# Shifting the start addresses of TensorE's operands in the feed-forward layers, by 64 bytes from set to set and 32 bytes from pair to pair

## The chip, the cores and the metric

The kernel runs on one core of a Trainium2 chip. The metric is the device time of one execution in microseconds (us). Before the change it is 2165.8 us, the median of two runs (2165.64 and 2165.96).

## What is computed

A trunk of two decoder layers over 256 tokens of width 2048, in float32. Cut to what matters here:

```python
for layer in range(2):
    hn = rms_norm(h, norm_mix[layer])
    h = h + (mlstm_mixer(hn, ...) if layer == 0 else rglru_mixer(hn, ...))
    hn = rms_norm(h, norm_ffn[layer])
    g, u = split(hn @ ffn_w_in[layer])          # 2048 x 11264
    h = h + (silu(g) * u) @ ffn_w_out[layer]    # 5632 x 2048
return rms_norm(h, norm_final)
```

Every product is a matrix of 256 tokens times a weight matrix that is read from HBM once.

## The kernel before

**Two halves of each operand.** TensorE multiplies in the type fp32r, which keeps fewer bits than float32. So each operand is split into a rounded part and a rest: ScalarE casts the raw value into the high half, VectorE subtracts that from the raw value and writes the low half (`split`, L205 to L207). A product is then three matmuls into the same PSUM bank: high by high, high by low, low by high (`block`, L258 to L260; `product`, L687 to L689; `mm_feat`, L275 to L277). The operand that lies still in the array while the other streams through it (the stationary one) is loaded by an LDWEIGHTS instruction ahead of each matmul.

**The feed-forward layer** (`ffn`, L671) runs over four chunks of hidden columns, of 3, 3, 3 and 2 blocks of 512. For each block, `hidden(j)` (L691) streams 8 weight tiles, called pairs p = 0 to 7 (`pairs`, L227). Five of them are plain: 24 matmuls of 512 columns each. Three (p = 1, 3, 5, `SEVENS`) use a scheme with seven products instead of eight, after sums of weights and of operands: 21 matmuls each. Behind each chunk `project_out` (L422) multiplies the block of hidden values with the second weight matrix, in four quarters q of 512 columns, through `linear_tok` (L250) and `stream4` (L215). In both, the weights are the moving operand (512 columns, 2048 bytes in each partition), and the tokens the stationary one (128 columns, 512 bytes).

**Where the operands lie.** `four` (L202) takes each of these weight tiles from a pool: 4 raw buffers, and 3 buffers each for the high halves (`whi`, and `whix` and `whit` for the seven products) and the low halves (`wlo`, `wlox`, `wlot`). All are 4 x 512 elements of 4 bytes, 8192 bytes in each partition, and follow one another. The stationary operands of `hidden` are written by `NormPairs.pair` (L374) into tiles `p0` to `p7` of 6144 or 7168 bytes (`p_f` in the profile). Those of `project_out` are `hh` and `hl`, written by `turn_v` (L732). The mixers have their own weight buffers, from the pool's tags in `stream` (L180), and their own stationary operands (`x_m`, `yh`, `yl`, `zh`, `zl`).

**What orders the work.** The program text gives the order on each engine; casts and subtractions of the weights are put ahead by a priority (`AHEAD`). Buffers in a pool rotate, and a writer waits until the last reader of the buffer is done. Work for the next stage (transposes, statistics) is kept in the list `pending` and taken out one at a time between weight tiles (`run_pending`, L175).

Of the kernel before, what the change touches and what calls it, by code (L numbers as in the profile page):

```python
# [8 lines left out]
F32 = mybir.dt.float32  # L9
F32R = mybir.dt.float32r  # L10
# [4 lines left out]
P = 128  # L15
T = 256
# [8 lines left out]
NB = 512  # L25
EPS = 1e-6
BIG = 1e30
AHEAD = 1000

SEVENS = (1, 3, 5)  # L30
PRODUCTS = (
# [7 lines left out]
def kernel(  # L39
# [23 lines left out]
    small = ctx.enter_context(tc.tile_pool(name="small", bufs=2))  # L63
# [14 lines left out]
    def pool_of(key):  # L78
        return pools[key][0]

    def acc(name):
        return pool_of("acc").tile([P, NB], F32, tag="bank", name=name)
# [67 lines left out]
    part, at, used = 0, 0, [0, 0, 0]  # L150
    for name, src, n in par_src:
        if part == 0 and at or at + n > P:
            part, at = part + 1, 0
# [26 lines left out]
    def stream(w, c0, nk, ncols=NB):  # L180
# [5 lines left out]
        for kg in range(0, nk, 2):  # L186
# [12 lines left out]
            for i in range(2):  # L199
                yield kg + i, hi[:, i, 0:ncols], lo[:, i, 0:ncols]  # L200

    def four(what, name, dtype, bufs):  # L202
        return pool_of("w").tile([P, 4, NB], dtype, tag=what, name=f"{what}{name}", bufs=bufs)

    def split(hi, lo, src):  # L205
        nc.scalar.copy(hi, src)  # L206
# [43 lines left out]
    def linear_tok(w, c0, nk, act, name, ncols=NB, lag=0):  # L250

        ps = [acc(f"{name}_{b}") for b in range(NT)]

        def block(b, k, hi, lo):
            ah, al = act(k)
            bs = slice(b * P, (b + 1) * P)
            o = ps[b][:, 0:ncols]
            nc.tensor.matmul(o, lhsT=ah[:, bs], rhs=hi, start=(k == 0), stop=False)  # L258
            nc.tensor.matmul(o, lhsT=ah[:, bs], rhs=lo, start=False, stop=False)  # L259
            nc.tensor.matmul(o, lhsT=al[:, bs], rhs=hi, start=False, stop=(k == nk - 1))  # L260

        late = []
        for k, hi, lo in stream(w, c0, nk, ncols):
            block(0, k, hi, lo)
            late.append((k, hi, lo))
            if len(late) > lag:
                block(1, *late.pop(0))
            if k > 1:
                run_pending()
        for kt in late:  # L270
            block(1, *kt)
        return ps
# [20 lines left out]
    class Norm:  # L293
# [62 lines left out]
        def finish(self):  # L356
            v = small.tile([P, NT], F32, tag="ms", name=f"ms_{self.name}")
            nc.vector.tensor_reduce(out=v, in_=self.ss, axis=mybir.AxisListType.X, op=ALU.add)
            nc.vector.tensor_scalar(out=v, in0=v, scalar1=1.0 / D, scalar2=EPS, op0=ALU.mult, op1=ALU.add)
            self.rstd = small.tile([P, NT], F32, tag="rstd", name=f"rstd_{self.name}")  # L360
            nc.gpsimd.tensor_tensor(self.rstd, v, mhalf[:, 0:NT], op=ALU.pow)
            if self.bcast:
                dg = small.tile([P, NT, P], F32, tag="dg", name=f"dg_{self.name}", bufs=1)
                for b in range(NT):
                    nc.vector.tensor_scalar_mul(dg[:, b, :], ident, self.rstd[:, b:b + 1])
                pb = misc(f"bc_{self.name}")
                nc.tensor.matmul(pb[:, 0:T], lhsT=ones, rhs=dg.rearrange("p b t -> p (b t)"), start=True, stop=True)
                self.bc = small.tile([P, T], F32, tag="rbc", name=f"rbc_{self.name}")
                nc.scalar.copy(self.bc, pb[:, 0:T])

    class NormPairs(Norm):


        def pair(self, p):  # L374
            plain = p not in SEVENS
            k0, k1 = 2 * p, 2 * p + 1
            order = ((k0, 0), (k0, 1), (k1, 0), (k1, 1)) if plain else ((k1, 1), (k0, 0), (k0, 1), (k1, 0))
            n = 6 if plain else 7
            pt = misc(f"tr_{self.name}{p}").rearrange("p (s t) -> p s t", t=P)
            for i, (k, b) in enumerate(order):  # L380
                nc.tensor.transpose(pt[:, i, :], h[:, b, k * P:(k + 1) * P], ident)
            c = pool_of("x").tile([P, 8, P], F32, tag="c", name=f"c_{self.name}{p}")
            for k, sl in ((k0, slice(0, 2)), (k1, slice(2, 4))) if plain else ((k0, slice(1, 3)), (k1, slice(0, 4, 3))):
                nc.scalar.activation(c[:, sl, :], pt[:, sl, :], AF.Copy, scale=self.gain[:, k:k + 1])
            if plain:
                nc.vector.tensor_tensor(c[:, 4:6, :], c[:, 0:4:2, :], c[:, 1:4:2, :], op=ALU.subtract)
                src = c[:, 0:6, :]
            else:

                nc.vector.tensor_tensor(  # L390
                    c[:, 4:6, :], c[:, 0:1, :].broadcast_to([P, 2, P]), c[:, 2:4, :], op=ALU.subtract
                )
                nc.vector.tensor_tensor(c[:, 6, :], c[:, 3, :], c[:, 4, :], op=ALU.subtract)
                nc.vector.tensor_tensor(c[:, 7, :], c[:, 1, :], c[:, 6, :], op=ALU.subtract)
                src = c[:, 1:8, :]
            xt = pool_of("x").tile([P, 2, n, P], F32R, tag=f"p{p}", name=f"p{p}_{self.name}")
            split(xt[:, 0], xt[:, 1], src)
            self.x.append(xt)

# [22 lines left out]
    def project_out(w, nk, act, nxt, last=True):  # L422

        for q in range(4):
            held = last and q == 3 and nxt.lag
            ps = linear_tok(w, q * NB, nk, act, f"po{q}", lag=nxt.lag if held else 0)
            for b in range(NT):
                hs = h[:, b, q * NB:(q + 1) * NB]
                nc.vector.tensor_tensor(hs, ps[b], hs, op=ALU.add)
                if held:  # L430
                    nxt.store(b)
            if last and q == 0:
                nxt.open()
            if last and not held:
                pending.extend(nxt.parts(q))
# [235 lines left out]
    def ffn(layer, n, nxt):  # L671

        w = ffn_w_in[layer]
# [10 lines left out]
        if True:  # L684
# [5 lines left out]

            def hidden(j):  # L691

                ps = {c: acc(f"{c}_{j}") for c, _, _ in PRODUCTS}
                started = set()
                dif = fp.tile([P, 2, NB], F32, tag="dif", name=f"dif{j}")
                sg = fp.tile([P, NT, NB], F32, tag="sg", name=f"sg{j}")
                for p, ops in pairs(w, j):
                    if p not in SEVENS:

                        for c, side, a in (("Q5", 1, 1), ("P2", 0, 0), ("Q3", 1, 2), ("P4", 0, 1)):  # L700
                            for f in range(2):
                                product(ps[c], n.plain(p, f)[a], ops[2 * side + f], c not in started,
                                        p == NK // 2 - 1 and f == 1)
                                started.add(c)
                    else:
                        seven = n.seven(p)
                        for c, a, b in PRODUCTS:
                            product(ps[c], seven[a], ops[b], c not in started,
                                    p == SEVENS[-1] and c in ("P7", "P1", "Q6"))
                            started.add(c)  # L710
                    if p == SEVENS[-1]:
                        nc.scalar.copy(sg[:, 0, :], ps["P1"])
                        nc.vector.tensor_tensor(dif[:, 0, :], ps["Q6"], sg[:, 0, :], op=ALU.subtract)
                        nc.vector.tensor_tensor(dif[:, 1, :], ps["P7"], dif[:, 0, :], op=ALU.add)
                    if p > 0:
                        run_pending()
                v = fp.tile([P, NT, NB], F32, tag="v", name=f"v{j}")
                for b in range(NT):
                    nc.vector.tensor_tensor(v[:, b, :], ps["Q5"], dif[:, b, :], op=ALU.add)
                nc.vector.tensor_tensor(sg[:, 0, :], ps["P2"], sg[:, 0, :], op=ALU.add)  # L720
                nc.scalar.activation(sg[:, 0, :], sg[:, 0, :], AF.Silu, scale=n.rstd[:, 0:1])
                nc.vector.tensor_tensor(v[:, 0, :], ps["Q3"], v[:, 0, :], op=ALU.add)
                nc.vector.tensor_tensor(sg[:, 1, :], ps["P4"], dif[:, 1, :], op=ALU.subtract)
                nc.scalar.activation(sg[:, 1, :], sg[:, 1, :], AF.Silu, scale=n.rstd[:, 1:2])
                for b in range(NT):
                    nc.vector.scalar_tensor_tensor(
                        out=v[:, b, :], in0=v[:, b, :], scalar=n.rstd[:, b:b + 1], in1=sg[:, b, :],
                        op0=ALU.mult, op1=ALU.mult,
                    )
                return v  # L730
# [38 lines left out]
    nc.vector.tensor_scalar_mul(nsp8, sp8, -1.0)  # L769

    n3 = NormPairs("f1", par["g_ffn"][:, 16:32])

    def rglru_mixer():
        rg = open_pool("rg", "rg")
# [187 lines left out]
```

## Time and profile before

| | |
|---|---|
| time of the profiled execution | 2165.18 us |
| its span, first to last instruction | 2163.4 us |
| median of the runs shown | 2165.8 us |
| TensorE (PE) busy | 2126.7 us, 98% of the span, 10658 matmuls |
| VectorE (DVE) busy | 1524.6 us, 70% |
| ScalarE (ACT) busy | 1071.0 us, 50% |
| DMA | 405.70 MB, mean 188 GB/s |

The span of the profiled execution is the time between its first and last instruction; 1.8 us of its time lie around it. Matmuls are pipelined: one starts while the one before still drains, so the durations of the rows (some 390 ns for 512 columns) overlap, and what a matmul costs is the distance from its start to the next one's start. That distance is read from the timeline, which gives each instruction's start.

### The profile page before, as it was taken

The numbers are of one execution on the slowest core, as the hardware profiler recorded it, in microseconds if no ns is written. First come the engines' busy times: TensorE is split into PE (matmuls) and PEld (weight loads), VectorE is DVE, ScalarE is ACT, GpSimd is POOL, SyncE is SP. The second block draws the span as 40 slices with busy tenths as digits, with TensorE's granted clock in tenths as the row PEclk, the third lists the DMA queues.
The fourth block names the chain that finished last, engine by engine and source line by source line (L and its number), as shares of the span: only waits on it lengthen the run. The fifth ranks groups of instructions, "written<-read, shape, count | busy, mean of one in ns | idle before, by whom it ended". The sixth has DMA issues, their size and how long they took to land.

```text
span 2163.4 us, 26826 instructions
## 1 busy us (share of the span) xinstructions
PE 2126.7 (98%) x10658; PEld 1788.9 (83%) x10658; DVE 1524.6 (70%) x1486; ACT 1071.0 (50%) x1040; POOL 43.4 (2%) x62
## 2 busy tenths in 40 slices
PE   8999999899999999999999999989999999999998
PEld 7988888788888888888879999778888888888886
DVE  5655555688578758866856786768857875886685
ACT  5444445555345435544544758555434543553444
POOL 0011110000000000000000000000000000000002
PEclk9999999999999999999999999999999999999999
DMA  6556655556555655565636665555665565556563
GB/s 209 166 163 178 180 180 185 178 202 209 189 193 188 203 186 195 195 201 188 206 106 195 194 188 188 190 176 195 214 195 194 175 214 175 194 195 213 176 214 117
DMA packets 211078, 405.70 MB, mean 188 GB/s; under 512 B 14520, under 2 KB 14728, under 8 KB 210824
## 3 DMA queue, kind: packets, MB, share of 16 engines
q1 hardware_dynamic: 210808, 402.94, 57.2%
q8 instruction: 83, 1.36, 0.3%
q10 hardware_dynamic: 144, 1.05, 0.1%
q14 instruction: 43, 0.35, 0.0%
HBM read 401.84 MB, written 2.10 MB: 187 GB/s over the span
## 4 chain that ended last, share of the span: by engine, by line
PE 91%; DVE 3%; ACT 2%; DMA 2%; issue 1%; SPq 0%; POOL 0%; ACTq 0%; DVEq 0%; POOLq 0%
PE po L259 10%; PE po L258 10%; PE po L260 10%; PE P L688 7%; PE P L689 7%; PE P L687 7%; PE Q L688 6%; PE Q L689 6%; PE Q L687 6%; DMA raw<-in_ffn_w_in_dram 2%; PE rec L277 1%; PE qk L275 1%; DVE wlo L207 1%; PE qk L276 1%; PE rec L276 1%; PE o L260 1%
## 5 line engine op out<-in xcount | busy, mean ns | idle before, releaser
L206 ACT CAST whi<-raw 128x2048 fp32r<-128x2048 f32 x198 | 378.3, 1912 | 465.8 <-PE P L689 204.4
L207 DVE TENSOR_TENSOR wlo<-raw,whi 128x2048 fp32r<-128x2048 f32 x198 | 451.8, 2295 | 204.8 <-ACT whi L206 204.6
L196 DVE TENSOR_TENSOR wlo<-raw,whi 128x1024 fp32r<-128x1024 f32 (+1 forms) x225 | 273.3, 1219 | 194.0 <-ACT whi L195 193.7
L195 ACT CAST whi<-raw 128x1024 fp32r<-128x1024 f32 (+1 forms) x225 | 234.3, 1047 | 215.8 <-PE po L260 53.2
L259 PE MATMUL po<-wlo,hh 128*128 128x512 f32 x704 | 275.2, 391 | 0.0
L258 PE MATMUL po<-whi,hh 128*128 128x512 f32 x704 | 275.0, 391 | 0.0
L260 PE MATMUL po<-whi,hl 128*128 128x512 f32 x704 | 273.6, 390 | 0.0
L206 ACT CAST whit<-sum 128x2048 fp32r<-128x2048 f32 x66 | 126.2, 1913 | 161.5 <-PE P L689 94.5
L207 DVE TENSOR_TENSOR wlot<-sum,whit 128x2048 fp32r<-128x2048 f32 x66 | 151.3, 2292 | 58.9 <-ACT whit L206 58.7
L687 PE MATMUL Q<-whi,p_f 128*128 128x512 f32 x440 | 175.7, 399 | 8.5 <-ACT whi L206 8.5
L688 PE MATMUL Q<-wlo,p_f 128*128 128x512 f32 x440 | 174.1, 396 | 3.6 <-DVE wlo L207 3.6
L687 PE MATMUL P<-whi,p_f 128*128 128x512 f32 x440 | 174.0, 395 | 0.0
L689 PE MATMUL Q<-whi,p_f 128*128 128x512 f32 x440 | 172.8, 393 | 0.0
L688 PE MATMUL P<-wlo,p_f 128*128 128x512 f32 x440 | 172.7, 393 | 0.0
L689 PE MATMUL P<-whi,p_f 128*128 128x512 f32 x440 | 172.5, 392 | 0.0
L258 PEld LDWEIGHTS po<-whi,hh 128*128 128x128 f32 x704 | 132.2, 188 | 27.5 <-ACT hh L439 0.3
L259 PEld LDWEIGHTS po<-wlo,hh 128*128 128x128 f32 x704 | 132.5, 188 | 26.5
L260 PEld LDWEIGHTS po<-whi,hl 128*128 128x128 f32 x704 | 132.1, 188 | 26.9
L206 ACT CAST whix<-raw 128x1536 fp32r<-128x1536 f32 x66 | 98.0, 1485 | 80.6 <-PE P L689 53.9
L207 DVE TENSOR_TENSOR wlox<-raw,whix 128x1536 fp32r<-128x1536 f32 x66 | 115.7, 1753 | 16.8 <-ACT whix L206 16.3
L687 PEld LDWEIGHTS Q<-whi,p_f 128*128 128x128 f32 x440 | 83.4, 190 | 26.6 <-ACT whi L206 9.1
L688 PEld LDWEIGHTS Q<-wlo,p_f 128*128 128x128 f32 x440 | 83.3, 189 | 24.4 <-DVE wlo L207 7.4
(261 smaller groups left out, 4258.5 us busy)
## 6 DMA issues: line engine op xcount, KB each, us to landing
raw<-in_ffn_w_in_dram SPq DMA_DIRECT2D x352, 512.0 KB, 4.8
raw<-in_ffn_w_out_dram SPq DMA_DIRECT2D x176, 512.0 KB, 4.9
raw<-in_m_w_in_dram SPq DMA_DIRECT2D x95, 512.0 KB, 3.8
raw<-in_r_w_in_dram SPq DMA_DIRECT2D x64, 512.0 KB, 4.2
raw<-in_m_w_out_dram SPq DMA_DIRECT2D x32, 512.0 KB, 3.7
raw<-in_r_w_out_dram SPq DMA_DIRECT2D x32, 512.0 KB, 3.7
gr<-in_r_gate_w_dram SPq DMA_DIRECT2D x8, 512.0 KB, 3.8
h<-in_x_dram SPq DMA_DIRECT2D x4, 512.0 KB, 7.9
```

The costliest lines, as they stand in the source:

```text
L195: nc.scalar.copy(hi[:, i:i + step, 0:ncols], r)
L196: nc.vector.tensor_tensor(lo[:, i:i + step, 0:ncols], r, hi[:, i:i + step, 0:ncols].bitcast(F32), op=ALU.subtract)
L206: nc.scalar.copy(hi, src)
L207: nc.vector.tensor_tensor(lo, src, hi.bitcast(F32), op=ALU.subtract)
L258: nc.tensor.matmul(o, lhsT=ah[:, bs], rhs=hi, start=(k == 0), stop=False)
L259: nc.tensor.matmul(o, lhsT=ah[:, bs], rhs=lo, start=False, stop=False)
L260: nc.tensor.matmul(o, lhsT=al[:, bs], rhs=hi, start=False, stop=(k == nk - 1))
L275: nc.tensor.matmul(o, lhsT=hi, rhs=ah, start=first_in_bank, stop=False, skip_group_check=True)
L276: nc.tensor.matmul(o, lhsT=hi, rhs=al, start=False, stop=False, skip_group_check=True)
L687: nc.tensor.matmul(o, lhsT=a[0], rhs=b[0], start=start, stop=False)
L688: nc.tensor.matmul(o, lhsT=a[0], rhs=b[1], start=False, stop=False)
L689: nc.tensor.matmul(o, lhsT=a[1], rhs=b[0], start=False, stop=stop)
```

## The change

The program computes the same values with the same instructions. What differs is where operands lie in SBUF.

- Each high or low half in the feed-forward layers gets a buffer of 8640 bytes instead of 8192, and the tile starts a multiple of 64 bytes into it. The multiple is a counter modulo 8. The counter goes up by one at each quarter of each `project_out` (the mixers' too, where it has no effect) and at each `hidden(j)`, so all tiles of one such set have one shift, and the next set the next.
- In the second layer each tile `p0` to `p7` is 32 bytes longer, so that each of them starts 32 bytes further than it would. In the first layer nothing is added.
- The tile `rbc`, 1024 bytes, has one buffer instead of two.

In the built program the operands start at these addresses, counted in bytes from a multiple of 512:

| operand | before | after |
|---|---|---|
| `whi`, `whix`, `whit` in the feed-forward layers, buffers 0, 1, 2 | 288, 288, 288 | 288, 224, 160, plus the set's shift |
| `wlo`, `wlox`, `wlot` there | 288, 288, 288 | 96, 32, 480, plus the set's shift |
| `hh`, `hl` | 288 | 416 |
| `p0` to `p7`, first layer | 480 | 480 |
| `p0` to `p7`, second layer | 480 | 224, 256, 288, 320, 352, 384, 416, 448 |
| `raw` | 288 | 288 |
| mixers: `x_m` and `yh`, `yl`, `zh`, `zl` | 480 and 288 | 480 and 288 |

The diff, cut to its core:

```diff
+PHASE = 16
...
+    phase = [0]
+
     def four(what, name, dtype, bufs):
-        return pool_of("w").tile([P, 4, NB], dtype, tag=what, name=f"{what}{name}", bufs=bufs)
+        pad = 7 * PHASE if dtype == F32R else 0
+        t = pool_of("w").tile([P, 4 * NB + pad], dtype, tag=what, name=f"{what}{name}", bufs=bufs)
+        at = phase[0] % 8 * PHASE if pad else 0
+        return t[:, at:at + 4 * NB].rearrange("p (a n) -> p a n", n=NB)
...
-                self.bc = small.tile([P, T], F32, tag="rbc", name=f"rbc_{self.name}")
+                self.bc = small.tile([P, T], F32, tag="rbc", name=f"rbc_{self.name}", bufs=1)
...
     class NormPairs(Norm):
+        pad = 0
...
-            xt = pool_of("x").tile([P, 2, n, P], F32R, tag=f"p{p}", name=f"p{p}_{self.name}")
+            xt = pool_of("x").tile([P, 2 * n * P + self.pad], F32R, tag=f"p{p}", name=f"p{p}_{self.name}")
+            xt = xt[:, 0:2 * n * P].rearrange("p (s i t) -> p s i t", s=2, t=P)
...
     # project_out
         for q in range(4):
+            phase[0] += 1
...
             def hidden(j):
+                phase[0] += 1
...
     n3 = NormPairs("f1", par["g_ffn"][:, 16:32])
+    n3.pad = PHASE // 2
```

The instructions on TensorE, VectorE, ScalarE and SyncE stand in the same order with the same waits. On GpSimd (POOL) one wait differs, at the second mixer's small memset of `rc` (the padded input of its convolution), because the buffer now lies over memory that TensorE read. Before:

```order
L361 TENSOR_TENSOR rstd_f_3744<-ms_f_3741,mhalf 128x2 [waits DVE_49]
L783 MEMSET rc_8492 128x4x3 [waits DMAHW1_49,DVE_49]
L783 MEMSET rc_9139 128x4x3 [waits DVE_49]
L361 TENSOR_TENSOR rstd_m_8570<-ms_m_8567,mhalf 128x2 [waits DVE_49]
L783 MEMSET rc_9751 128x4x3 [waits DVE_49,Pool_49]
```

And now, in the same place of the same queue (line numbers are 13 or 7 higher):

```order
L368 TENSOR_TENSOR rstd_f_3744<-ms_f_3741,mhalf 128x2 [waits DVE_49]
L796 MEMSET rc_8492 128x4x3 [waits DMAHW1_49,DVE_49,PE_49]
L796 MEMSET rc_9139 128x4x3
L368 TENSOR_TENSOR rstd_m_8570<-ms_m_8567,mhalf 128x2 [waits DVE_49]
L796 MEMSET rc_9751 128x4x3 [waits DVE_49,Pool_49]
```

The first memset waits for TensorE too, and the second for nothing of its own.

## The prediction, made before the changed kernel ran

> **What bounds the kernel now.** I read the page's first part and its chain of waits, then the costliest groups, then the timeline of TensorE.
>
> ```profile
> PE 2126.7 (98%) x10658; PEld 1788.9 (83%) x10658; DVE 1524.6 (70%) x1486; ACT 1071.0 (50%) x1040; POOL 43.4 (2%) x62
> ...
> PEclk9999999999999999999999999999999999999999
> ...
> PE 91%; DVE 3%; ACT 2%; DMA 2%; issue 1%; SPq 0%; POOL 0%; ACTq 0%; DVEq 0%; POOLq 0%
> ...
> L206 ACT CAST whi<-raw 128x2048 fp32r<-128x2048 f32 x198 | 378.3, 1912 | 465.8 <-PE P L689 204.4
> L207 DVE TENSOR_TENSOR wlo<-raw,whi 128x2048 fp32r<-128x2048 f32 x198 | 451.8, 2295 | 204.8 <-ACT whi L206 204.6
> ...
> L258 PE MATMUL po<-whi,hh 128*128 128x512 f32 x704 | 275.0, 391 | 0.0
> ...
> L687 PE MATMUL Q<-whi,p_f 128*128 128x512 f32 x440 | 175.7, 399 | 8.5 <-ACT whi L206 8.5
> L688 PE MATMUL Q<-wlo,p_f 128*128 128x512 f32 x440 | 174.1, 396 | 3.6 <-DVE wlo L207 3.6
> ```
>
> TensorE is busy for 98% of the span at the full granted clock, and the chain that ended last is TensorE for 91%. ScalarE and VectorE wait for TensorE to free their buffers (465.8 us of ScalarE's idle time before the casts, mostly until a matmul ended), while TensorE waits for them in these groups for 8.5 and 3.6 us in all. So the end is set by how fast one matmul follows another, and an address can only matter there. A row's 391 ns is latency; the pace is the distance between starts. The timeline of TensorE in stretches without a break, the first and last row of each:
>
> ```profile
> 619.71 0.39 PE L687 MATMUL Q<-whi,p_f 128*128 128x512 f32 x1
> 619.94 0.39 PE L688 MATMUL Q<-wlo,p_f 128*128 128x512 f32 x1
> ...
> 640.99 0.39 PE L687 MATMUL Q<-whi,p_f 128*128 128x512 f32 x1
> ```
>
> ```profile
> 574.73 0.39 PE L258 MATMUL po<-whi,hh 128*128 128x512 f32 x1
> ...
> 595.81 0.39 PE L258 MATMUL po<-whi,hh 128*128 128x512 f32 x1
> ```
>
> The first stretch (first layer, `hidden`) has 94 rows, 93 steps in 21.28 us: 228.8 ns each. The second (`project_out`) has 94 rows too, 21.08 us: 226.7 ns. Both are matmuls of 512 columns from the same buffers, and the two paces hold over the whole program (20.37 us for 89 steps from 1849.62, 20.18 us for 89 steps from 1989.65). Is it the code or the address? The mixer answers, where one helper (`linear_tok`) runs with one set of weight buffers, first on `x_m`, then on `yh`:
>
> ```profile
> 274.65 0.39 PE L258 MATMUL v<-whi,x_m 128*128 128x512 f32 x1
> ...
> 286.79 0.39 PE L260 MATMUL v<-whi,x_m 128*128 128x512 f32 x1
> ```
>
> ```profile
> 322.80 0.39 PE L258 MATMUL po<-whi,yh 128*128 128x512 f32 x1
> ...
> 337.98 0.39 PE L259 MATMUL po<-wlo,yh 128*128 128x512 f32 x1
> ```
>
> 53 steps in 12.14 us are 229.1 ns; 67 steps in 15.18 us are 226.6 ns. `x_m` and `p_f` start 480 bytes past a multiple of 512, `yh` and `hh` 288, and the moving weights 288 in all four. So the pace goes with the place of the stationary operand against the moving one: 0 bytes apart 226.7, 192 bytes apart 228.9. That is the effect that this change plays on, and it is 1%.
>
> **Other distances.** The feature-wise products (256 columns, weights stationary) show two more. `qk`, `rec` and `gb` have their stationary operand 320 bytes past the moving one (modulo 512), `rg` 384:
>
> ```profile
> 1164.79 0.28 PE L276 MATMUL gb<-x_m,whi 128*128 128x256 f32 x1
> ...
> 1180.99 0.28 PE L275 MATMUL gb<-x_m,whi 128*128 128x256 f32 x1
> ```
>
> ```profile
> 83.82 0.28 PE L276 MATMUL qk<-x_m,whi 128*128 128x256 f32 x1
> ...
> 99.96 0.28 PE L275 MATMUL qk<-x_m,whi 128*128 128x256 f32 x1
> ```
>
> ```profile
> 1303.76 0.28 PE L276 MATMUL rg<-rvl,ghi 128*128 128x256 f32 x1
> ...
> 1309.93 0.28 PE L277 MATMUL rg<-rvh,glo 128*128 128x256 f32 x1
> ```
>
> `gb`: 143 steps in 16.20 us, 113.3 ns, exactly half of 226.7. `qk`, at the same addresses: 137 steps in 16.14 us, 117.8. `rg`: 52 steps in 6.17 us, 118.7. So the floor is 0.443 ns per column, and what the address adds to a matmul is 0 (distance 0), 2.1 ns (192), 0 or 4.5 ns (320; the slow pace holds for some 300 of the 2304 matmuls of `qk`, `rec` and `gb`, so 0.6 on the mean), and 5.4 ns (384). I do not know the mechanism; that one distance has two paces says that it is a matter of phase, into which a steady row of matmuls can fall or not.
>
> **The change, part by part.** *Where it acts.* `hidden` has 22 sets (2 layers, 11 blocks) of 5 plain pairs of 24 matmuls and 3 of 21: 22 x 183 = 4026. `project_out` in the two layers has three groups of 704: 2112. The mixers' operands keep their distances. After the change the three buffers of a half start at three different places, high and low halves lie 192 bytes apart (modulo 512), and the set's shift goes through all eight multiples of 64. So in the first layer every distance that is a multiple of 64 occurs about equally often, in the second layer's `hidden` every multiple of 32.
>
> *Its price.* No row has these mixtures, so the cost of a matmul is bounded by the rows above: 0 at the floor, 5.4 ns as in `rg`, or 10.8 ns if what `rg` shows is a price per column and a matmul of 512 columns pays twice. I take the mean over the four distances that the trace has, (0 + 2.1 + 0.6 + 5.4) / 4 = 2.0 ns, since the change spreads the distances evenly and nothing singles one out. Then `hidden` changes by 4026 x (2.0 - 2.1) = -0.4 us and `project_out` by 2112 x 2.0 = +4.2 us: +3.8 us. What `hidden` gains by leaving a middling place, `project_out` loses by leaving the best one. At the bounds: all at the floor, -4026 x 2.1 = -8.5 us; all at 5.4, 4026 x 3.3 + 2112 x 5.4 = +24.7 us; all at 10.8, 4026 x 8.7 + 2112 x 10.8 = +57.8 us.
>
> *The casts, subtractions and loads* write and read the same bytes at other places. I cost that at nothing: the groups L206 and L207 above have 465.8 and 204.8 us of idle time before them. The raw buffers, which the transfers fill, stay at 288. Were the cover gone, each cast that ends 100 ns late could hold TensorE as long, 330 casts 33 us; nothing points to it.
>
> *The memset of* `rc` *and the single* `rbc` *buffer* cost nothing either.
>
> ```profile
> L783 POOL MEMSET rc<- x4: 110/110/113, 1067.0 to 1228.5; 128x12 f32 x4
> ```
>
> ```profile
> POOL rstd_m L361 <- DVE ms_m L359: 69.2, 2, 48.9
> ```
>
> The first memset takes 110 ns at 1067.0 us, after `wlot` of the last hidden block was written. Now it also waits until TensorE has read that block, a few us later. Behind it on POOL stands the second mixer's `rstd_m`, ahead of which POOL waited 48.9 us for VectorE; the second memset needs no wait. The first `rbc` was last read in the first mixer, and the next is written in the second.
>
> The sum on the profiled execution: 2165.18 + 3.8 = 2169.0 us, the span 2163.4 + 3.8 = 2167.2. The median of the runs is 0.6 us above that execution, so I forecast 2169.6 us. A measurement of this kernel can tell about 2% (43 us) from no change; this is within it.
>
> **The rivals.** *A: addresses do nothing* and the two paces come from something that goes with the operands. For it: the same addresses gave 113.3 and 117.8 in the mixers. Against it: `v` and `po` above, one helper and one set of weight buffers. It gives 2165.8 us. The Trainium skill speaks for it (SBUF — State Buffer, Who interferes with whom): TensorE reads its moving operand and its weights through two independent ports and waits for nobody. By that rule the sum is zero, also 2165.8; the steps of 229.1 and 226.6 ns are hard to fit into it.
>
> *B: faster, the conflict is broken up.* If 192 bytes is a rare bad place and most others are like 0 and like `gb`, then `hidden` falls to the floor and `project_out` stays there: 2165.8 - 8.5 = 2157.3 us. For it: `rec` and `gb` run at the floor at a third distance. Against it: `rg` does not.
>
> *C: slower, the phase never settles.* Before, all matmuls of a stretch had their moving operand at one place modulo 512, and could fall into step. Now the place jumps by 192 or 320 bytes at nearly every matmul, between high and low half. If the steps never settle, all pay what `rg` pays, the shortest rows of matmuls here: +24.7 us, 2190.5. It decides if the mean cost in `hidden` and `project_out` is above some 4 ns. At twice that price (C2) it is 2223.6 us, over 2% slower.
>
> *D: the floor itself goes.* The change puts the stationary tiles of the second layer's odd pairs on multiples of 64, where before every such operand lay 32 past one. 11 x (3 x 21 + 24) = 957 matmuls are touched. How far below 226.7 a step can go no row here says; if it were by the 5.4 ns that the worst distance costs, from 228.8 to 221.3, it would be 957 x 7.5 = 7.2 us, 2158.6 with the rest unchanged, and more if the moving operand follows. The Trainium skill (TensorE: Matmul & The Clock Gate, Wait — 56ns, not 53.3ns?) has a warm step of N / 2.4 GHz + 2.5 ns for bf16, an estimate of 215.8 ns at 512 columns; no step of 512 columns in this trace reaches it.
>
> **How the numbers follow.** Forecast (2163 to 2178, the mean price between 0.5 and 3.5 ns) 0.42; A 0.15; B 0.15; C 0.20; C2 0.03; D 0.05. The range of 2156 to 2192 takes in A, B, C and the usual size of D, and leaves out C2 and the tails. Slower by over 2% needs C2 or a worse C, 0.04; faster by over 2% needs D with all operands following it, 0.02; within 2% is 0.94.
>
> **What would show it.** Right: in the timeline after, steps of `project_out` vary from set to set and average 228 to 230 ns instead of 226.7; those of `hidden` average near 228.8, some sets at the floor, some worse; the groups of ScalarE and VectorE keep their 1912 and 2295 ns; the mixers do not change. A shows as 228.8 and 226.7 unchanged in every set. B shows as 226.7 everywhere, C as 231 to 232 everywhere with no set at the floor, D as steps below 226 in the second layer alone. The prediction is wrong if the difference lies in idle time before TensorE's groups, or outside the feed-forward layers.

## The result, and the profile after

The changed kernel takes 2186.6 us (median of 2186.37 and 2186.86) against 2165.8: a ratio of 1.0093, 95% interval 1.0068 to 1.0117. It is slower by 0.9%, within the 2% and within the range of 2156 to 2192, but the forecast was +3.8 us and the measurement is +20.8.

The page of the kernel after:

```profile
PE 2147.3 (98%) x10658; PEld 1788.8 (82%) x10658; DVE 1524.9 (70%) x1486; ACT 1069.9 (49%) x1040; POOL 43.4 (2%) x62
...
PEclk9999999999999999999999999999999999999999
...
PE 91%; DVE 3%; ACT 2%; DMA 2%; issue 1%; SPq 0%; POOL 0%; ACTq 0%; DVEq 0%; POOLq 0%
...
L213 ACT CAST whi<-raw 128x2048 fp32r<-128x2048 f32 x198 | 377.4, 1907 | 480.8 <-PE P L700 222.0
L214 DVE TENSOR_TENSOR wlo<-raw,whi 128x2048 fp32r<-128x2048 f32 x198 | 451.6, 2293 | 213.1 <-ACT whi L213 212.8
...
L265 PE MATMUL po<-whi,hh 128*128 128x512 f32 x704 | 278.7, 396 | 0.0
...
L698 PE MATMUL Q<-whi,p_f 128*128 128x512 f32 x440 | 176.4, 401 | 8.8 <-ACT whi L213 8.8
L699 PE MATMUL Q<-wlo,p_f 128*128 128x512 f32 x440 | 175.0, 398 | 4.4 <-DVE wlo L214 4.4
```

TensorE's busy time grew by 20.6 us (2126.7 to 2147.3) and the span by 21.2 (2163.4 to 2184.6). The casts and subtractions did not get slower (1907 and 2293 ns, before 1912 and 2295), they only wait longer for TensorE, and TensorE waits for them hardly longer than before (8.8 and 4.4 us, before 8.5 and 3.6). So the matmuls themselves follow one another more slowly. Where, the start of the second layer's `hidden` tells. The timeline of before:

```profile
1436.55 0.80 PE L687 MATMUL Q<-whi,p_f 128*128 128x512 f32 x1 [4.09 <-ACT whi L206]
```

and of after:

```profile
1447.36 0.79 PE L698 MATMUL Q<-whi,p_f 128*128 128x512 f32 x1 [4.38 <-ACT whi L213]
```

10.8 us are lost by then, with the first layer, and the other 10.4 in the second. The timeline of after in stretches without a break, first and last row: `hidden` of the first layer, `project_out`, and `v` in the mixer.

```profile
619.65 0.40 PE L698 MATMUL Q<-whix,p_f 128*128 128x512 f32 x1
...
641.00 0.39 PE L700 MATMUL Q<-whix,p_f 128*128 128x512 f32 x1
```

```profile
579.74 0.40 PE L267 MATMUL po<-whi,hl 128*128 128x512 f32 x1
...
600.86 0.40 PE L265 MATMUL po<-whi,hh 128*128 128x512 f32 x1
```

```profile
274.73 0.39 PE L265 MATMUL v<-whi,x_m 128*128 128x512 f32 x1
...
286.87 0.39 PE L267 MATMUL v<-whi,x_m 128*128 128x512 f32 x1
```

92 steps in 21.35 us: 232.1 ns, before 228.8. 91 steps in 21.12 us: 232.1 ns, before 226.7. `v` keeps its 229.1 (53 steps, 12.14 us). Over the whole trace, the steps without a break average between 231.3 and 232.8 ns in every one of the 22 sets of `hidden` (229.0 before), and about 232.1 in `project_out` (227.0 before). With 4026 x 3.1 and 2112 x 5.1 that is 12.5 + 10.8 = 23 us, of which 21 reach the end. That every set, whatever its shift, pays the same is the sign that the prediction gave for rival C.

### The profile page after: what moved, and what is told of

It reads as the page before. It is cut to its first block, busy times and chain, and to the rows that moved or that the text cites. A ratio compares the mean times of both kernels' runs of the same rounds, so it can differ in the third digit from the quotient of the medians.

```text
span 2184.6 us, 26826 instructions
## 1 busy us (share of the span) xinstructions
PE 2147.3 (98%) x10658; PEld 1788.8 (82%) x10658; DVE 1524.9 (70%) x1486; ACT 1069.9 (49%) x1040; POOL 43.4 (2%) x62
## 4 chain that ended last, share of the span: by engine, by line
PE 91%; DVE 3%; ACT 2%; DMA 2%; issue 1%; SPq 0%; POOL 0%; ACTq 0%; DVEq 0%; POOLq 0%
PE po L265 10%; PE po L267 10%; PE po L266 10%; PE P L700 7%; PE P L699 7%; PE P L698 7%; PE Q L699 6%; PE Q L700 6%; PE Q L698 6%; DMA raw<-in_ffn_w_in_dram 2%; PE qk L282 1%; PE rec L284 1%; PE qk L283 1%; PE qk L284 1%; PE v L265 1%; PE o L267 1%
## 5 line engine op out<-in xcount | busy, mean ns | idle before, releaser
L213 ACT CAST whi<-raw 128x2048 fp32r<-128x2048 f32 x198 | 377.4, 1907 | 480.8 <-PE P L700 222.0
L214 DVE TENSOR_TENSOR wlo<-raw,whi 128x2048 fp32r<-128x2048 f32 x198 | 451.6, 2293 | 213.1 <-ACT whi L213 212.8
```

The lines of the kernel that those rows point to most:

```text
L214: nc.vector.tensor_tensor(lo, src, hi.bitcast(F32), op=ALU.subtract)
```

## The experiments

The theories at the start. **Jump**: the moving operand's start jumps from matmul to matmul, between buffers and between high and low half, and a step cannot settle. **Distance**: what counts is how far the stationary operand's start is from the moving one's, modulo some power of two; the old kernel had two good distances, and the change spreads them over mostly bad ones. Distances below are stationary minus moving start. Edits are against the changed kernel unless another is named; each time is the median, with the ratio to the kernel before on the same chip (before: 2167.4, 2167.4 and 2167.0 us in the three groups of runs).

### One place for a whole set, swept through 16 places

```diff
-        pad = 7 * PHASE if dtype == F32R else 0
+        pad = 128 if dtype == F32R else 0
-        at = phase[0] % 8 * PHASE if pad else 0
+        at = phase[0] % 16 * 8 if pad else 0
-    n3.pad = PHASE // 2
+    n3.pad = 0
```

> High and low halves are shifted together in steps of 32 bytes from set to set, through 16 places, and the buffers are a multiple of 512 bytes long, so that the moving operand starts at one place modulo 512 throughout a set; the second layer's operands are as before. The jump theory (a step that never settles because the moving operand's start jumps between matmuls): no set is above 229 ns by more than the breaks in it, sets at distance 0 are at 226.7, and the time is between 2155 and 2170 us. The distance theory (most distances are bad, and the mean over them is 232.1 ns): the sets differ widely, some at 226.7 and some above 236, their mean is 232, and the time is about 2187 us.

2187.4 us, ratio 1.0089 (1.0076 to 1.0103). Nothing jumps here within a set, and yet it is as slow as the change. Three quarters of one `project_out` that follow each other, at distances 0, 224 and 192 modulo 256:

```profile
761.81 0.39 PE L265 MATMUL po<-whi,hh 128*128 128x512 f32 x1
...
773.82 0.39 PE L267 MATMUL po<-whi,hl 128*128 128x512 f32 x1
...
777.74 0.39 PE L266 MATMUL po<-wlo,hh 128*128 128x512 f32 x1
...
789.88 0.39 PE L267 MATMUL po<-whi,hl 128*128 128x512 f32 x1
...
794.74 0.39 PE L267 MATMUL po<-whi,hl 128*128 128x512 f32 x1
...
806.87 0.39 PE L266 MATMUL po<-wlo,hh 128*128 128x512 f32 x1
```

53 steps in 12.01 us are 226.6 ns, 52 in 12.14 us are 233.5, 53 in 12.13 us are 228.9. The same over all sets of this run, from the starts in the trace, without the first dozen steps of a set or behind a break, and without steps over 250 ns:

| distance modulo 256, bytes | 0 | 32 | 64 | 96 | 128 | 160 | 192 | 224 |
|---|---|---|---|---|---|---|---|---|
| step of 512 columns, ns | 226.7 | 233.4 | 233.3 | 234.3 | 232.4 | 233.3 | 228.8 | 233.3 |

`hidden` (stationary at 480) and `project_out` (at 288) give the same step to within 0.3 ns at each of the seven distances that both have here (192 occurs in `project_out` alone), so it is the difference that counts, not either address. Both theories held something wrong: the distance theory expected single sets above 236 ns and none is; the jump theory is wrong in that constant places are slow too. But the main point is clear. Six of the eight distances cost 5.7 to 7.6 ns, and the old kernel had the two others: 0 in `project_out`, 192 in `hidden`.

### Buffers of 8640 bytes, without a shift

```diff
-        at = phase[0] % 8 * PHASE if pad else 0
+        at = 0
-    n3.pad = PHASE // 2
+    n3.pad = 0
```

> The buffers of 8640 bytes stay, so that the three buffers of a half and the two halves start at different places modulo 512, but no set is shifted and the second layer's operands are as before. Jump theory: all sets near 232 ns as in the change, 2186 us. Distance theory: the first layer and project_out still meet six distances in each set, so about 232 too; but always the same six, so that the mean may be off by 2 ns either way: 2174 to 2199 us. A rotation that matters by itself (the shift from set to set): 2166 us.

2186.3 us, ratio 1.0087 (1.0073 to 1.0101). The longer buffers alone give the whole loss; the shift from set to set and the second layer's pairs add nothing to it. It does not tell the theories apart, since both foresaw it.

### Only the second layer's operands

```diff
-        pad = 7 * PHASE if dtype == F32R else 0
+        pad = 0
```

> Only the second layer's operands are moved, by 32 bytes from pair to pair; all weight buffers are as before. Jump theory: the moving operand never jumps, so each pair settles within some matmuls at 226.7 to 229 ns by its distance; the second layer's hidden blocks change by less than 4 us, the rest not at all: 2162 to 2168 us. Distance theory: the second layer's hidden blocks go to 232 ns on the mean, 2013 x 3.3 = +6.6 us: 2172 us.

2171.9 us, ratio 1.0019 (1.0010 to 1.0028): +4.5 us where the moving operand does not jump at all. In the timeline, most of pair p4 (distance 64) and the first rows of p5 (distance 96) in the second layer:

```profile
1659.70 0.39 PE L699 MATMUL P<-wlo,p_f 128*128 128x512 f32 x1
...
1663.90 0.39 PE L699 MATMUL P<-wlox,p_f 128*128 128x512 f32 x1
```

18 steps in 4.20 us: 233.3 ns, as in the sweep. Over the whole layer the steps average 232.1 ns, and its pairs p0 (distance 192) and p2 (distance 0) are the only ones below 232, at 229.3 and 227.8 with their first steps. The distance alone lengthens the step here; the jump theory in its strict form falls.

But the distance does not fix the step by itself. In the first layer of this run every operand starts where it did before, modulo 512 (distance 192), and yet most of the first block of `hidden` and part of the second ran so:

```profile
418.15 0.40 PE L700 MATMUL P<-whi,p_f 128*128 128x512 f32 x1
...
468.09 0.40 PE L700 MATMUL P<-whit,p_f 128*128 128x512 f32 x1
```

These are 214 steps in 49.94 us without a break, 233.3 ns each, where the kernel before has 229.0. Behind the next break the run is back at 229.0. So at the same addresses a row of matmuls can hold one of two paces; what picks it, no run here shows. In the profiled execution it costs some 0.9 us (214 x 4.3 ns).

### `hidden` at distance 0

```diff
-        pad = 7 * PHASE if dtype == F32R else 0
+        pad = 128 if dtype == F32R else 0
-        at = phase[0] % 8 * PHASE if pad else 0
+        at = phase[0] if pad else 0
...
     # project_out
-            phase[0] += 1
+            phase[0] = 0
...
     # hidden
-                phase[0] += 1
+                phase[0] = 48
...
-    n3.pad = PHASE // 2
+    n3.pad = 0
```

> In hidden the weight halves start 192 bytes further, at the place of the stationary operands modulo 512 (distance 0), in project_out as before (distance 0 too); buffers are a multiple of 512 bytes long, nothing jumps within a stage. Both theories of the pace: hidden falls from 229.0 to 226.7 ns, 4026 x 2.2 = -9 us, 2157 us. If the place of the stationary operand alone sets the pace, hidden stays at 229 and the time at 2166 us.

2158.9 us, ratio 0.9959 (0.9946 to 0.9971), and in a second series on another chip 2160.7, ratio 0.9973 (0.9964 to 0.9982; that run's expectation is below). This beats both kernels. In the timeline of `hidden`:

```profile
619.77 0.39 PE L699 MATMUL Q<-wlo,p_f 128*128 128x512 f32 x1
...
640.85 0.39 PE L699 MATMUL P<-wlo,p_f 128*128 128x512 f32 x1
```

93 steps in 21.08 us, 226.7 ns instead of 228.8: moving the weights by 192 bytes is all that was needed. The stationary tiles lie where they lay, so the third case, in which the stationary place alone sets the pace, is excluded.

### Two places 256 bytes apart

```diff
 against the kernel with hidden at distance 0
-        at = phase[0] if pad else 0
+        at = (phase[0] + (what == "wlo") * 64) if pad else 0
```

> As the kernel with hidden at distance 0, but each low half lies 256 bytes further than its high half, so that the moving operand's start jumps by 256 bytes at nearly every matmul. If the distance counts modulo 256, and a jump by itself costs nothing: 227 ns everywhere as without the jump, about 2159 us. If it is the jump that keeps the step from settling: about 232 ns everywhere, 2187 us. If the distance counts modulo 512 and not 256: matmuls with the low half go to about 233 ns, the others stay, 2159 + 6138 / 3 x 6.3 = 2172 us.

2161.6 us, ratio 0.9973 (0.9963 to 0.9983).

```profile
619.70 0.39 PE L700 MATMUL P<-whit,p_f 128*128 128x512 f32 x1
...
640.77 0.39 PE L700 MATMUL Q<-whi,p_f 128*128 128x512 f32 x1
```

93 steps in 21.07 us, 226.6 ns. A jump of 256 bytes is no jump: the distance counts modulo 256.

### Two good places in turn

```diff
 against the kernel with hidden at distance 0
-        at = phase[0] if pad else 0
+        at = (phase[0] + (what == "wlo") * 16) if pad else 0
```

> As the kernel with hidden at distance 0, but each low half lies 64 bytes further, so that the moving operand alternates between the two places found good, distance 0 (226.7 ns) and 192 (229.0 ns). If each matmul pays its own distance: (2 x 226.7 + 229.0) / 3 = 227.5 ns, 2159 + 6138 x 0.8 = 2164 us. If alternating keeps the step from settling: about 232 ns, 2159 + 6138 x 5.3 = 2191 us.

2187.0 us, ratio 1.0092 (1.0077 to 1.0107).

```profile
619.80 0.40 PE L699 MATMUL Q<-wlox,p_f 128*128 128x512 f32 x1
...
640.92 0.40 PE L700 MATMUL Q<-whix,p_f 128*128 128x512 f32 x1
```

91 steps in 21.12 us: 232.1 ns, though each matmul on its own has distance 0 or 192, the two best. So the jump does cost after all, at 64 bytes where 256 cost nothing: a good distance is worth its price only in a row of matmuls that all have it. The two theories are one: in every row with a short step here, the place relative to each other repeats from matmul to matmul (modulo 256), at one of a few distances.

### Both operands on multiples of 256

```diff
 against the kernel with hidden at distance 0
-        pad = 128 if dtype == F32R else 0
+        pad = 64 if dtype == F32R else 0
-            xt = pool_of("x").tile([P, 2 * n * P + self.pad], F32R, tag=f"p{p}", name=f"p{p}_{self.name}")
-            xt = xt[:, 0:2 * n * P].rearrange("p (s i t) -> p s i t", s=2, t=P)
+            xt = pool_of("x").tile([P, 2 * n * P + 64], F32R, tag=f"p{p}", name=f"p{p}_{self.name}")
+            xt = xt[:, 8:8 + 2 * n * P].rearrange("p (s i t) -> p s i t", s=2, t=P)
...
     # hidden
-                phase[0] = 48
+                phase[0] = 56
```

> As the kernel with hidden at distance 0, but in hidden both operands start on a multiple of 256, where all moving and stationary operands before lay 32 past a multiple of 64. If the floor of 226.7 ns is one of address: the steps of hidden fall below 226, by 5 ns 20 us, 2139 us, and more if they reach 216 ns. If only the distance counts: 227 ns, about 2159 us.

2161.4 us, ratio 0.9974 (0.9963 to 0.9984).

```profile
619.81 0.39 PE L700 MATMUL P<-whit,p_f 128*128 128x512 f32 x1
...
640.89 0.39 PE L700 MATMUL Q<-whi,p_f 128*128 128x512 f32 x1
```

93 steps in 21.08 us, again 226.7 ns. Moving both operands onto multiples of 256 changed nothing, and the floor stays.

### Steps of 4 bytes

```diff
 against the kernel with hidden at distance 0
-    phase = [0]
+    phase = [0, 0, 0]
...
     # project_out
-            phase[0] = 0
+            phase[0] = phase[2] % 16
+            phase[2] += 1
...
     # hidden
-                phase[0] = 48
+                phase[0] = 48 + phase[1] % 16
+                phase[1] += 1
```

> As the kernel with hidden at distance 0, but the weight halves of each set lie 0 to 60 bytes further in steps of 4, one shift for a set, so that one run shows how wide the good place is. If both operands are read in blocks of 32 or 64 bytes and only the block counts: sets shifted by 0 to 28 or so stay at 227 ns and the rest go to 233, about 2159 + 6138 x 6.5 / 2 = 2179 us. If the distance must be met to the byte: only the sets without a shift stay at 227, all others are at 233, 2159 + 6138 x 6.5 x 15 / 16 = 2196 us.

2190.2 us, one run. Neither expectation holds. The moving operand 20, 28 and 12 bytes further than at distance 0:

```profile
564.84 0.40 PE L265 MATMUL po<-whi,hh 128*128 128x512 f32 x1
...
575.79 0.40 PE L266 MATMUL po<-wlo,hh 128*128 128x512 f32 x1
...
598.74 0.39 PE L265 MATMUL po<-whi,hh 128*128 128x512 f32 x1
...
609.89 0.39 PE L266 MATMUL po<-wlo,hh 128*128 128x512 f32 x1
...
615.83 0.39 PE L699 MATMUL Q<-whi,p_f 128*128 128x512 f32 x1
...
636.88 0.39 PE L701 MATMUL Q<-whi,p_f 128*128 128x512 f32 x1
```

46 steps in 10.95 us are 238.0 ns, 49 in 11.15 us 227.6, 92 in 21.05 us 228.8. Over the sets of `hidden` the step goes 227.2, 237.3, 233.3, 228.9, 231.7, 238.6, 233.5, 227.7 ns for shifts of 0, 4, 8, 12, 16, 20, 24 and 28 bytes: neither a wide good place nor a single one. 20 bytes off is the worst seen, 11.9 ns above the floor.

### The mixers' operands too

```diff
 against the kernel with hidden at distance 0, in Norm.quarter
-            xt = pool_of("x").tile([P, 4, 2, T], F32R, tag=f"x{q}", name=f"x{q}_{self.name}")
+            xt = pool_of("x").tile([P, 8 * T + 64], F32R, tag=f"x{q}", name=f"x{q}_{self.name}")
+            xt = xt[:, 16:16 + 8 * T].rearrange("p (k s t) -> p k s t", s=2, t=T)
```

> As the kernel with hidden at distance 0, and the operands x of both mixers lie 64 bytes further too, so that v, o (distance 192 before) and qk, rec, gb (distance 64 modulo 256) come to distance 0; rg stays. If the distance acts in the mixers as in the feed-forward layers: v and o fall from 229.1 to 226.7, 768 x 2.4 = 1.8 us, and the 256-column matmuls run at 113.3 throughout, up to 2304 x 0.7 = 1.6 us: some 3 us below the kernel with hidden at distance 0. If the 256-column matmuls follow another rule: 1 to 2 us below it.

> The kernel with hidden at distance 0 once more, on the same chip as its version for the mixers: 0.4% below the kernel before, as in its first run.

The mixers' version takes 2170.2 us, ratio 1.0014 (1.0005 to 1.0023): 9.5 us above the kernel without this edit on the same chip, where 3 below were expected. That kernel itself came out 0.3% below the kernel before, not the 0.4% expected. Two stretches, `gb` and `v`:

```profile
1164.79 0.28 PE L284 MATMUL gb<-x_m,wlo 128*128 128x256 f32 x1
...
1180.99 0.28 PE L284 MATMUL gb<-x_m,wlo 128*128 128x256 f32 x1
```

```profile
274.63 0.39 PE L267 MATMUL v<-whi,x_m 128*128 128x512 f32 x1
...
286.88 0.39 PE L267 MATMUL v<-whi,x_m 128*128 128x512 f32 x1
```

`v` falls from 229.1 to 226.9 ns (54 steps, 12.25 us), as foreseen. But `gb`, 113.3 before, goes to 120.0 ns (135 steps, 16.20 us), and `qk` and `rec` hold 120 ns in nearly all their steps too. For 256 columns distance 0 is a bad one and 64 a better one (113.3 ns, in some rows 117.8); for 512 columns it is the other way round. The price of a distance belongs to a shape.

## Why the prediction was right and wrong

**Right: what the change acts on.** That the end is set by the step from matmul to matmul, that the step depends on the operands' places relative to each other, that `project_out` would lose a good place, and that casts, subtractions, transfers and mixers would not move: the page and the timeline after show each of these. Slower within 2% is what came. But the band that it held likeliest, 2163 to 2178 us at 0.42, was missed, and so were its signs, an average of 228 to 230 ns in `project_out` and of near 228.8 in `hidden`. That the time lies in the stated range is owed to its width, which took in rival C at 0.20.

**Wrong: the mean price.** The step that failed is "the mean over the four distances that the trace has, (0 + 2.1 + 0.6 + 5.4) / 4 = 2.0 ns, since the change spreads the distances evenly and nothing singles one out". It measured 232.1 - 226.7 = 5.4 ns. Two things were wrong in it. The first two of the four, the only ones of 512 columns, were no sample: the sweep shows that they are the two best of eight. The last two were of 256 columns, and do not carry over: distance 64 (320 modulo 256) costs `gb` nothing and a matmul of 512 columns 6.6 ns. And the calculation let each matmul pay for its own distance. With the sweep's prices for the multiples of 64 (226.7, 233.3, 232.4, 228.8) it gives (0 + 6.6 + 5.7 + 2.1) / 4 = 3.6 ns, still short of 5.4. The rest goes with the mixing, whose price the kernel with two good places in turn shows. In the second layer's `hidden`, where the other multiples of 32 occur too, the mean over all eight prices is 5.2 ns, and 5.7 were measured (232.4 ns); there the mixing adds little.

**The terms.** A matmul of `hidden` was to get 0.1 ns shorter, 0.4 us in all; it got 3.1 ns longer, some 12.5 us. One of `project_out` was to get 2.0 ns longer, 4.2 us in all; it got 5.1 longer, some 10.8 us.

**The rivals.** C was nearest, in its price (the 5.4 ns of `rg`), its sign (231 to 232 ns everywhere) and its time (2190.5 against 2186.6). Its reason holds only in part: constant places are slow too, if they are the wrong ones. A, addresses that do nothing, falls with the sweep, and with it the zero that followed from the Trainium skill (SBUF — State Buffer, Who interferes with whom): no other thing than an address changed there, and the step went from 226.7 to 233.4 ns. B had the sign wrong: 192 bytes is no rare bad place, but the second best of eight. D falls with the operands on multiples of 256, which stay at 226.7 ns.

**A cost at nothing for the wrong reason.** The waits on POOL in the kernel after:

```profile
POOL rc L796 <- PE po L266: 730.5, 1, 730.5
```

The memset of `rc` waited not "a few us" but until the last `project_out`, and ran at 1137.4 us instead of 1067.0. It still cost nothing, since `rstd_m` behind it was not due before 1145.7 us; but 8 us of cover were left, not 49.

**Open.** By what mechanism the distance sets the step, whether it is the weight load that meets the moving stream, and why the price changes between 256 and 512 columns, no run here shows. Nor was it pursued that one address pattern can have two paces: 113.3 and 117.8 ns in the mixers (`gb` has 3 of its steps at 116 to 119 ns in the kernel before, and 194 of 764 in the one with longer buffers and no shift, at the same places modulo 512), and 229.0 and 233.3 ns in `hidden`. The prices of the sweep are those of the rows that ran there, most distances in a few sets.

## What to carry to other kernels

Where TensorE is the bound, read the distance between starts in a long stretch for each group, beside where its two operands start in memory; a per cent or two may lie there, and padding that seems harmless can take it away. Keep the place of the moving operand relative to the stationary one constant through a stage (buffer lengths that are multiples of 256 bytes did this here), then choose that place by a sweep in one run with one shift for each set. Sweep each shape by itself, and don't take the places that a trace happens to have as a sample of the others.

## What the runs showed of the hardware

- The step of fp32r matmuls of 512 columns goes from 226.7 to 238.6 ns with the operands' places; for these places 256 bytes are a full round (226.6 ns with a jump of 256 between high and low half), and 4 bytes already count (227.2 ns at distance 0, 237.3 with the moving operand 4 bytes further).
- No place tried gave a step below 226.7 ns for 512 columns or 113.3 for 256, which is the same 0.443 ns per column.
- Alternating between two places with steps of 226.7 and 228.8 ns gives 232.1, more than either.
- At the same places modulo 512 (distance 192) 512 columns ran at 229.0 ns in most rows and at 233.3 in one row of 214 steps.
- At one distance (0) 512 columns run at the floor and 256 columns at 120.0 ns instead of 113.3.
